# Weight loads in pieces of 4 KB per partition, in one pool of twelve buffers shared with the split's remainders

## The chip, the cores and the metric

The kernel runs on one core of a Trainium2 chip, in one launch. The metric is the device time of one execution in microseconds (us); the time of a kernel is the median of its runs. The engines are TensorE (PE in the profile; PEld is its weight load), VectorE (DVE), ScalarE (ACT), GpSimd (POOL) and SyncE (SP), which here does little but issue DMA transfers.

## The reference

Two layers act on 256 tokens of width 2048, with 256 tokens of context beside them in the first layer. Each layer first computes a modulation from the condition vector, the product of a silu vector with a 2048 by 6144 matrix, which yields a shift, a scale and a gate. Layer 0 projects to the parts of a gated linear attention and of a short convolution, mixes, and projects back; layer 1 projects to a pooled branch and a gate, mixes, and projects back. After each layer comes a normalised sum. Cut to that:

```
for i in range(2):
    sh, sc, gt = split(silu(c) @ w_ada[i] + b_ada[i], 3)        # (2048) @ (2048, 6144)
    u = x * (1 + sc) + sh                                       # (256, 2048)
    if i == 0:
        uc = ctx * (1 + sc_c) + sh_c                            # context, the same w_ada[0]
        s_f, s_b = context_states((uc @ w_in_e)[:, k, v, gates])
        y = even_mixer(u @ w_in_e, s_f, s_b, ...) @ w_out_e     # w_in_e (2048, 8224)
    else:
        xp, gate = split(u @ w_in_o, 2)                         # w_in_o (2048, 4096)
        z = einsum(window_mean(xp) - xp, w_pool) * pool_scale
        y = (z * silu(gate)) @ w_out_o
    x = layer_norm(sqrt(2) * x + gt * y)
```

All of it is fp32, with some 250 MB of weights that are each read once.

## The kernel before

**Products.** An fp32 product is made of three matmuls of rounded operands: `mm3` (lines 188 to 192) multiplies wh by uh (L190), the remainder wl by uh (L191) and wh by ul (L192). A weight therefore goes through three steps. `load_unit` (L135) loads a unit of four k-tiles of 128 rows by 512 columns, 1 MB, into one buffer `raw` of 8 KB per partition (L138, on the SP queue). `split_unit` (L143) cuts it in halves of two k-tiles: ScalarE casts a half to `wh` (L152), VectorE subtracts to get the remainder `wl` (L153). Then TensorE has 12 matmuls of 128x512 for each half and each block of tokens. For a few units marked wide the halves go to other buffers, `swh` and `swl`.

**Buffers.** `wraw` has 4 buffers of 8 KB per partition, one for each unit whatever its size, `whp` 4 of 4 KB and `wlp` 4 of 4 KB. A load into a buffer waits until the last reader of the unit four back is done.

**Order.** The list `specs` holds all units in the order of their use. `w_next` hands out the parts of the next one, and through `w_ahead` and `w_load` has the units behind it loaded (two ahead) and split (one ahead). Each engine's order is that of a list scheduler, which places instructions by priority and by its own idea of when each can start, the state of the pools included. The order below is therefore that of the built programs.

**Modulation.** The rows of layer 0 that are needed first are made on TensorE, straight from fp32 weights: `mod_rows` (L263) loads 1 MB units of `w_ada` and multiplies the silu vector with each k-tile (L274, tile `ada`). All other parts of the modulation are made on VectorE: `ada_unit` (L479) loads a 1 MB unit of `w_ada`, and `ada_accum` adds its four k-tiles, times a scalar, to `aacc` (L532 the first, L534 the others). These units use the same buffers `raw` and run through the whole kernel, a few at a time between blocks of the products (`pump_ada`).

**Stages.** Nine stages of one or two k-tiles each (`STAGES`) load modulation rows, make u, and multiply with the key columns (`stage_u`, `stage_k`, `v_fill`). Then come the rest of `w_in_e` (tile `xacc`, with the attention and the convolution in the background), `w_out_e` (`oacc`), layer 1 (`w_in_o`, `w_pool`), and `w_out_o`. Two places matter below. L966 on VectorE scales an attention output `y` that TensorE then transposes (L974, tile `yT`). L1333 multiplies a gate by a pooled branch, and TensorE transposes the result (L1286, tile `y1T`).

Of the kernel before, what the change touches and what calls it, by code (L numbers as in the profile page):

```python
# [9 lines left out]
F32 = mybir.dt.float32  # L10
F32R = mybir.dt.float32r
I32 = mybir.dt.int32
AF = mybir.ActivationFunctionType
ALU = mybir.AluOpType
# [3 lines left out]
P = 128  # L18
D = 2048
KT = D // P  # L20
SEQ = 256
NSLOT = 31
TAU = 16.0
EPS = 1e-5
ALPHA = math.sqrt(2.0)
# [5 lines left out]
KRAW = False  # L31
# [29 lines left out]
def kernel(  # L61
# [24 lines left out]
    nc = tc.nc  # L86
    names = {}

    def nm(s):
        names[s] = names.get(s, 0) + 1  # L90
        return f"{s}_{names[s]}"

    cpool = ctx.enter_context(tc.tile_pool(name="cpool", bufs=1))
    wraw = ctx.enter_context(tc.tile_pool(name="wraw", bufs=4))
    whp = ctx.enter_context(tc.tile_pool(name="whp", bufs=4))
    wlp = ctx.enter_context(tc.tile_pool(name="wlp", bufs=4))
    s4p = ctx.enter_context(tc.tile_pool(name="s4p", bufs=NSLOT))
    accp = ctx.enter_context(tc.tile_pool(name="accp", bufs=4, space=PSUM))
    mpp = ctx.enter_context(tc.tile_pool(name="mpp", bufs=4, space=PSUM))
# [9 lines left out]
    def const(shape, dt, name):  # L109
        return cpool.tile(shape, dt, tag=name, name=name)  # L110

    def slot(shape, dt=F32, name="s"):
        return s4p.tile(shape, dt, tag="s4", name=nm(name))

    def mp(shape, name="mp"):
        return mpp.tile(shape, F32, tag="mp", name=nm(name))
# [4 lines left out]
    def raw_tile(shape, name="raw"):  # L121
        return wraw.tile(shape, F32, tag="raw", name=nm(name))
# [10 lines left out]


    def load_unit(src, k0, nk, n0, nw=512):  # L135
        small_ = KRAW and nk * nw <= 1024
        r = slot([P, nk, nw], F32, "kraw") if small_ else raw_tile([P, nk, nw])
        nc.sync.dma_start(  # L138
            r, src[k0 * P : (k0 + nk) * P, n0 : n0 + nw].rearrange("(k p) n -> p k n", p=P)
        )  # L140
        return r

    def split_unit(r, nk, wide=False):  # L143
        parts = []
        for j in range(0, nk, 2):
            w = min(2, nk - j)
            if wide:
                h, l = slot([P, w, 512], F32R, "swh"), slot([P, w, 512], F32R, "swl")
            else:
                h = whp.tile([P, w, 512], F32R, tag="wh", name=nm("wh"))  # L150
                l = wlp.tile([P, w, 512], F32R, tag="wl", name=nm("wl"))
            nc.scalar.copy(h, r[:, j : j + w, :])  # L152
            nc.vector.tensor_tensor(out=l, in0=r[:, j : j + w, :], in1=h.bitcast(F32), op=ALU.subtract)  # L153
            for i in range(w):
                parts.append((h[:, i, :], l[:, i, :]))
        return parts
# [3 lines left out]
    wide = set()  # L160
# [70 lines left out]
    sil = const([P, KT, 34], F32, "sil")  # L231
# [31 lines left out]
    def mod_rows(k0, n):  # L263

        nw = n * P
        ps = mp([P, nw], "ada")
        nk = 2048 // nw
        for half, c0 in ((0, D + k0 * P), (1, k0 * P)):
            for kk in range(0, KT, nk):
                r = load_unit(w_ada[0], kk, nk, c0, nw)  # L270
                for j in range(nk):
                    kt = kk + j
                    g = kt % 4
                    nc.tensor.matmul(  # L274
                        out=ps[32 * g : 32 * g + 32, :], lhsT=sil[:, kt, 2 - 2 * half : 34 - 2 * half], rhs=r[:, j, :],
                        start=half == 0 and kt < 4, stop=half == 1 and kt >= KT - 4,
                    )
        return ps
# [37 lines left out]
    k0 = 0  # L316
# [35 lines left out]
    for s in ODD:  # L352
        g = int(s[1])
# [125 lines left out]
    def ada_unit(layer, k0, n0):  # L479

        if not ADA_SLOT:
            r = load_unit(w_ada[layer], k0, 4, n0)
            return [r[:, j, :] for j in range(4)]
        q = {"s": nc.sync, "g": nc.gpsimd}[ADA_SLOT]
        parts = []
        for k in (k0, k0 + 2):
            r = slot([P, 2, 512], F32, "araw")
            q.dma_start(r, w_ada[layer][k * P : (k + 2) * P, n0 : n0 + 512].rearrange("(k p) n -> p k n", p=P))
            parts += [r[:, 0, :], r[:, 1, :]]
        return parts  # L490
# [75 lines left out]
    prev, k0 = None, 0  # L566
# [135 lines left out]
    def gate_gen():  # L702
# [8 lines left out]
        for hp in range(2):  # L711
            res = {}
            for d in range(2):
# [22 lines left out]
                for half in range(2):  # L736
# [19 lines left out]
                    yield 1800  # L756
                nc.scalar.activation(e, e, AF.Exp, scale=-1.0 / TAU)
                nc.vector.tensor_tensor(out=e, in0=e, in1=kTc[hp], op=ALU.mult)
# [43 lines left out]
    def gla_gen(hp):  # L802
# [7 lines left out]
        def exps(t):  # L810
            nc.scalar.activation(t, t, AF.Exp, scale=-1.0 / TAU)

# [3 lines left out]
        def sub(o, a, b):  # L816
            nc.vector.tensor_tensor(out=o, in0=a, in1=b, op=ALU.subtract)
# [70 lines left out]
        sub(ch(kb), ch(gb)[:, :, 0:1].to_broadcast([P, 16, 64]), ch(gb))  # L888
        nc.scalar.activation(gl, gf[:, :, 63::64], AF.Exp, scale=-1.0 / TAU)
        nc.scalar.activation(bl, gb[:, :, ::64], AF.Exp, scale=-1.0 / TAU)  # L890
        for t, w in ((kf, kt_), (kb, kt_), (gf, qt), (gb, qt)):
# [169 lines left out]
    for i in range(2):  # L1061
        n0 = i * 512
        u = slot([P, 2, 512], F32, "ca")
        g = slot([P, 2, 512], F32, "cg")
# [237 lines left out]
    for s in ODD:  # L1302
        g = int(s[1])
# [84 lines left out]
```

## Time and profile before

| | |
|---|---|
| time, median of 3 runs | 1009.52 us (1008.19 to 1010.95) |
| profiled execution | 1010.29 us, of which the span from first to last instruction is 1008.5 us |
| mean granted clock of TensorE | 0.991 |
| busy in the span: PE, DVE, ACT | 960.9, 801.6, 469.3 us |
| moved by DMA | 255.44 MB, 253 GB/s in the mean |
| q1, the queue of SP | 72.4% of the time of 16 DMA engines |

Busy is the time in which an engine has an instruction running; what is left of the span is waiting. The chain that ended last is followed back from the last instruction, at each step to what released it. "[2.54 <-DMA raw<-in_w_ada_dram]" behind a row means that the engine stood idle for 2.54 us before it, until a transfer into `raw` had landed. The DMA share is the mean busy share of 16 DMA engines; transfers that overlap on an engine can take it above 1.

### The profile page before, as it was taken

The page shows a single profiled execution, that of the slowest core. Times are in us where ns is not written, and L with a number is a line of the kernel's source. Part 1 is how long each engine was busy: PE and PEld are TensorE (multiplying, and loading weights), DVE is VectorE, ACT ScalarE, POOL GpSimd, SP SyncE. Part 2 cuts the span into 40 slices and gives each one's busy share as a digit, 9 for nine tenths or more (in the row PEclk, how much of TensorE's full clock was granted, in tenths as well). Part 3 has the DMA queues.
Part 4 walks back from the last instruction along what each step waited for, and adds up shares of the span by engine and source line. Part 5 has one row for each costly group of instructions (what it writes and reads, how often), then busy time and mean ns, then how long its engine had stood idle before and what let it go on. Part 6 is the DMA issues. An engine that isn't in the chain of part 4 may idle for free.

```text
span 1008.5 us, 14323 instructions
## 1 busy us (share of the span) xinstructions
PE 960.9 (95%) x5654; PEld 759.2 (75%) x5654; DVE 801.6 (79%) x1142; ACT 469.3 (47%) x643; POOL 24.4 (2%) x56
## 2 busy tenths in 40 slices
PE   5899999999999999999999899999999999989995
PEld 4566656778878877887878778888778778778885
DVE  1555546979996999779999688897979997666676
ACT  2422214356675676236454344445745555435340
POOL 2000000000000000000000000000010001000000
PEclk9999999999999999999999999999999999999998
DMA  9977889566787586867767877985497999875532
GB/s 265 329 263 262 276 284 336 193 243 231 258 302 252 188 269 219 257 206 274 241 228 234 284 255 247 353 298 207 152 368 275 304 334 322 278 266 203 174 119 83
DMA packets 150371, 255.44 MB, mean 253 GB/s; under 512 B 5078, under 2 KB 46720, under 8 KB 150304
## 3 DMA queue, kind: packets, MB, share of 16 engines
q1 hardware_dynamic: 146592, 245.13, 72.4%
q0 software_dynamic: 2896, 8.72, 2.7%
q10 hardware_dynamic: 816, 0.68, 0.3%
q8 instruction: 44, 0.72, 0.3%
q14 instruction: 23, 0.19, 0.0%
HBM read 252.41 MB, written 2.10 MB: 252 GB/s over the span
## 4 chain that ended last, share of the span: by engine, by line
PE 41%; DVE 33%; DMA 18%; issue 5%; ACT 3%; SPq 0%; DVEq 0%; ACTq 0%
DMA raw<-in_w_ada_dram 15%; DVE wl L153 11%; DVE aacc L534 9%; PE oacc L191 5%; PE oacc L192 5%; PE oacc L190 5%; DMA raw<-in_w_in_o_dram 3%; PE xacc L192 3%; PE xacc L191 3%; PE xacc L190 3%; PE ada L274 2%; PE kacc L190 2%; PE kacc L192 2%; PE kacc L191 2%; PE pr L406 1%
## 5 line engine op out<-in xcount | busy, mean ns | idle before, releaser
L152 ACT CAST wh<-raw 128x1024 fp32r<-128x1024 f32 (+1 forms) x250 | 257.0, 1044 | 252.6 <-PE xacc L192 77.9
L153 DVE TENSOR_TENSOR wl<-raw,wh 128x1024 fp32r<-128x1024 f32 (+1 forms) x250 | 297.3, 1210 | 49.3 <-ACT wh L152 47.1
L534 DVE SCALAR_TENSOR_TENSOR aacc<-raw,sil,aacc 128x512 f32<-128x512 f32 x240 | 179.0, 747 | 34.2 <-DMA raw<-in_w_ada_dram 30.7
L190 PE MATMUL xacc<-wh,uxh 128*128 128x512 f32 x384 | 153.8, 400 | 0.0
L191 PE MATMUL xacc<-wl,uxh 128*128 128x512 f32 x384 | 150.9, 393 | 0.9 <-DVE wl L153 0.9
L192 PE MATMUL xacc<-wh,uxl 128*128 128x512 f32 x384 | 151.1, 394 | 0.0
L191 PEld LDWEIGHTS xacc<-wl,uxh 128*128 128x128 f32 x384 | 72.6, 189 | 17.3 <-DVE wl L153 1.7
L190 PEld LDWEIGHTS xacc<-wh,uxh 128*128 128x128 f32 x384 | 72.5, 189 | 15.6 <-issue 0.5
L192 PEld LDWEIGHTS xacc<-wh,uxl 128*128 128x128 f32 x384 | 72.4, 188 | 15.6 <-issue 0.2
L426 DVE TENSOR_TENSOR knat<-kacc,knat 128x512 f32<-128x512 f32 x64 | 42.8, 685 | 35.8 <-PE kacc L192 35.6
L285 ACT COPY arow<-ada 128x256 f32<-128x256 f32 (+1 forms) x9 | 3.1, 349 | 101.9 <-PE ada L274 101.9
L274 PE MATMUL ada<-raw,sil 128*32 128x256 f32 (+1 forms) x576 | 36.2, 380 | 12.0 <-DMA raw<-in_w_ada_dram 12.0
L190 PE MATMUL xacc<-wh,u1h 128*128 128x512 f32 x112 | 44.8, 400 | 0.8 <-ACT u1h L1167 0.8
L190 PE MATMUL oacc<-wh,y1h 128*128 128x512 f32 (+1 forms) x120 | 45.5, 379 | 0.0
L192 PE MATMUL oacc<-wh,y1l 128*128 128x512 f32 (+1 forms) x120 | 45.0, 375 | 0.0
L191 PE MATMUL oacc<-wl,y1h 128*128 128x512 f32 (+1 forms) x120 | 45.0, 375 | 0.0
L191 PE MATMUL xacc<-wl,u1h 128*128 128x512 f32 x112 | 44.1, 394 | 0.3 <-DVE wl L153 0.3
L192 PE MATMUL xacc<-wh,u1l 128*128 128x512 f32 x112 | 44.0, 393 | 0.0
L274 PEld LDWEIGHTS ada<-raw,sil 128*32 128x32 f32 x576 | 17.0, 118 | 28.6 <-issue 12.3
L190 PE MATMUL kacc<-wh,uxh 128*128 128x512 f32 x64 | 26.8, 418 | 1.5 <-ACT uxh L398 1.5
L1228 PE MATMUL xacc<-wh,dm 128*128 128x512 f32 x64 | 26.2, 409 | 1.6 <-ACT wh L152 1.6
L190 PE MATMUL kacc<-wh,uch 128*128 128x512 f32 x64 | 26.4, 412 | 0.5 <-DVE knat L426 0.5
(339 smaller groups left out, 1865.0 us busy)
## 6 DMA issues: line engine op xcount, KB each, us to landing
raw<-in_w_ada_dram SPq DMA_DIRECT2D x96, 1024.0 KB, 6.3
raw<-in_w_in_e_dram SPq DMA_DIRECT2D x54, 1024.0 KB, 6.0
raw<-in_w_in_o_dram SPq DMA_DIRECT2D x32, 1024.0 KB, 7.1
raw<-in_w_out_e_dram SPq DMA_DIRECT2D x16, 1024.0 KB, 6.7
raw<-in_w_out_o_dram SPq DMA_DIRECT2D x16, 1024.0 KB, 5.1
raw<-in_w_in_e_dram SPq DMA_DIRECT2D x18, 512.0 KB, 7.2
raw<-in_w_pool_dram SPq DMA_DIRECT2D x4, 1024.0 KB, 7.5
gt<-in_b_ada_dram POOLq DMA_DIRECT2D x8, 256.0 KB, 3.8
```

The source lines that it names most:

```text
L152: nc.scalar.copy(h, r[:, j : j + w, :])
L153: nc.vector.tensor_tensor(out=l, in0=r[:, j : j + w, :], in1=h.bitcast(F32), op=ALU.subtract)
L190: nc.tensor.matmul(out=acc, lhsT=uh, rhs=wh, start=start, stop=False)
L191: nc.tensor.matmul(out=acc, lhsT=uh, rhs=wl, start=False, stop=False)
L192: nc.tensor.matmul(out=acc, lhsT=ul, rhs=wh, start=False, stop=stop)
L274: nc.tensor.matmul(out=ps[32 * g : 32 * g + 32, :], lhsT=sil[:, kt, 2 - 2 * half : 34 - 2 * half], rhs=r[:, j, :], start=half == 0 and kt ...
L285: arow_ins.append(nc.scalar.copy(a[:, :nw], ps))
L406: nc.tensor.matmul(out=pr[32 * g : 32 * g + 32, :], lhsT=wr[:, kk, :], rhs=quad_u[kk // 2][:, kk % 2, :], start=True, stop=True,)
L426: nc.vector.tensor_tensor(out=dst, in0=acc, in1=dst, op=ALU.add)
L534: e.scalar_tensor_tensor(out=a, in0=r[j], scalar=sc, in1=a, op0=ALU.mult, op1=ALU.add)
L1228: nc.tensor.matmul(out=accs[0], lhsT=dh, rhs=wh, start=f, stop=False)
```

## The change

A load unit is cut into pieces of 1024 elements (4 KB) per partition, 512 KB each; each piece has a buffer of its own and a DMA of its own. `wraw` holds 12 such buffers instead of 4 of 8 KB. The pool `wlp` is gone: remainders `wl` take buffers of `wraw`, under the same tag, so that pieces and remainders follow one another through the same twelve. The memory is the same, 48 KB per partition. `split_unit` casts and subtracts a piece as it did a half, in instructions of the same shapes and number; `mod_rows` and `ada_unit` find their k-tiles in the pieces. A unit of one or two k-tiles of 512 columns (256 or 512 KB, in the stages) stays one piece. SP issues 482 DMAs instead of 265. Line numbers of the changed kernel are 2 or 3 higher.

```
-    wraw = ctx.enter_context(tc.tile_pool(name="wraw", bufs=4))
+    wraw = ctx.enter_context(tc.tile_pool(name="wraw", bufs=NRAW))      # NRAW = 12
     whp = ctx.enter_context(tc.tile_pool(name="whp", bufs=4))
-    wlp = ctx.enter_context(tc.tile_pool(name="wlp", bufs=4))
...
     def load_unit(src, k0, nk, n0, nw=512):
-        small_ = KRAW and nk * nw <= 1024
-        r = slot([P, nk, nw], F32, "kraw") if small_ else raw_tile([P, nk, nw])
-        nc.sync.dma_start(
-            r, src[k0 * P : (k0 + nk) * P, n0 : n0 + nw].rearrange("(k p) n -> p k n", p=P)
-        )
-        return r
+        w = 1024 // nw
+        pieces = []
+        for k in range(k0, k0 + nk, w):
+            n = min(w, k0 + nk - k)
+            r = raw_tile([P, n, nw])
+            nc.sync.dma_start(r, src[k * P : (k + n) * P, n0 : n0 + nw].rearrange("(k p) n -> p k n", p=P))
+            pieces.append((r, n))
+        return pieces
...
-    def split_unit(r, nk, wide=False):
+    def split_unit(pieces, nk, wide=False):
         parts = []
-        for j in range(0, nk, 2):
-            w = min(2, nk - j)
+        for r, w in pieces:
...
-                l = wlp.tile([P, w, 512], F32R, tag="wl", name=nm("wl"))
-            nc.scalar.copy(h, r[:, j : j + w, :])
-            nc.vector.tensor_tensor(out=l, in0=r[:, j : j + w, :], in1=h.bitcast(F32), op=ALU.subtract)
+                l = wraw.tile([P, w, 512], F32R, tag="raw", name=nm("wl"))
+            nc.scalar.copy(h, r)
+            nc.vector.tensor_tensor(out=l, in0=r, in1=h.bitcast(F32), op=ALU.subtract)
...
 # mod_rows
-                r = load_unit(w_ada[0], kk, nk, c0, nw)
+                r = [p[:, i, :] for p, w in load_unit(w_ada[0], kk, nk, c0, nw) for i in range(w)]
...
-                        ... rhs=r[:, j, :],
+                        ... rhs=r[j],
...
 # ada_unit
-            r = load_unit(w_ada[layer], k0, 4, n0)
-            return [r[:, j, :] for j in range(4)]
+            return [p[:, i, :] for p, w in load_unit(w_ada[layer], k0, 4, n0) for i in range(w)]
```

With other loads and other buffers the scheduler also orders the engines anew. Three places show it; the order on TensorE, VectorE and ScalarE differs in many more.

TensorE in the early stages, where `mod_rows` takes its units; `ada` is the modulation of one stage, `kacc` the key columns. Before, in the fourth of the two-k-tile stages:

```order
L274 MATMUL ada_883<-raw_884,sil 32x256 x8
L274 MATMUL ada_883<-raw_894,sil 32x256 x8
L190 MATMUL kacc_954<-wh_870,uxh_120 128x512
L191 MATMUL kacc_954<-wl_871,uxh_120 128x512
L192 MATMUL kacc_954<-wh_870,uxl_121 128x512
```

and now, at the end of the same stage's modulation:

```order
L277 MATMUL ada_912<-raw_939,sil 32x256 x4
L194 MATMUL kacc_1047<-wl_906,uch_119 128x512
L195 MATMUL kacc_1047<-wh_905,ucl_120 128x512
L277 MATMUL ada_912<-raw_949,sil 32x256 x4
L277 MATMUL ada_912<-raw_951,sil 32x256 x4
L291 MATMUL adaT_963<-sel_101,arow_961 128x4 x2
```

A row "x8" was one unit, two of them stood together at the head of a stage. Now a piece is "x4", and the first five or six pieces of a stage stand apart, with three to five matmuls of 128x512 between them; the uninterrupted runs of such rows are 40 instead of 26.

VectorE in the last part of the attention, where the norm's root (`rst`, `rsy`) is followed by `y` (before):

```order
L1015 TENSOR_TENSOR rsy_2_4885<-rsy_2_4885,rst_2_4884 128x4
L534 SCALAR_TENSOR_TENSOR aacc_10_4985<-raw_5082,sil,aacc_10_4985 128x512
L966 SCALAR_TENSOR_TENSOR y_4859<-po_4861,rsy_2_4885,gs_2936 128x256 x2
L966 SCALAR_TENSOR_TENSOR y_4859<-po_4872,rsy_2_4885,gs_2936 128x256
L153 TENSOR_TENSOR wl_5040<-raw_5000,wh_5039 128x1024
L153 TENSOR_TENSOR wl_5044<-raw_5000,wh_5043 128x1024
L966 SCALAR_TENSOR_TENSOR y_4859<-po_4872,rsy_2_4885,gs_2936 128x256
```

and now:

```order
L1016 TENSOR_SCALAR rst_2_5113<-rst_2_5113 128x4
L1017 TENSOR_TENSOR rsy_2_5114<-rsy_2_5114,rst_2_5113 128x4
L968 SCALAR_TENSOR_TENSOR y_5088<-po_5090,rsy_2_5114,gs_3073 128x256 x2
L968 SCALAR_TENSOR_TENSOR y_5088<-po_5101,rsy_2_5114,gs_3073 128x256 x2
L980 SCALAR_TENSOR_TENSOR ybl_5087<-yT_5265,colT,ybh_5086 128x2x128
L156 TENSOR_TENSOR wl_5332<-raw_5286,wh_5331 128x1024
L980 SCALAR_TENSOR_TENSOR ybl_5087<-yT_5265,colT,ybh_5086 128x2x128
L536 SCALAR_TENSOR_TENSOR aacc_10_5220<-raw_5323,sil,aacc_10_5220 128x512 x2
```

The first k-tile of a `w_ada` unit stood ahead of `y`; now two remainders stand within the root's steps, and the k-tiles of `w_ada` behind `y`.

VectorE in layer 1, at the second of three gates multiplied by a pooled branch (before):

```order
L153 TENSOR_TENSOR wl_7382<-raw_7345,wh_7381 128x1024
L153 TENSOR_TENSOR wl_7418<-raw_7385,wh_7417 128x1024
L534 SCALAR_TENSOR_TENSOR aacc_16_7330<-raw_7471,sil,aacc_16_7330 128x512
L153 TENSOR_TENSOR wl_7422<-raw_7385,wh_7421 128x1024
L1333 TENSOR_TENSOR gate_7258<-gate_7258,pooled_7039 128x1024
L534 SCALAR_TENSOR_TENSOR aacc_16_7330<-raw_7471,sil,aacc_16_7330 128x512 x2
```

and now:

```order
L536 SCALAR_TENSOR_TENSOR aacc_16_7715<-raw_7716,sil,aacc_16_7715 128x512
L536 SCALAR_TENSOR_TENSOR aacc_16_7715<-raw_7718,sil,aacc_16_7715 128x512 x2
L156 TENSOR_TENSOR wl_7769<-raw_7732,wh_7768 128x1024
L1335 TENSOR_TENSOR gate_7639<-gate_7639,pooled_7406 128x1024
L156 TENSOR_TENSOR wl_7773<-raw_7734,wh_7772 128x1024
L536 SCALAR_TENSOR_TENSOR aacc_16_7715<-raw_7760,sil,aacc_16_7715 128x512 x2
```

The k-tile of a new unit (`raw_7471`) stood ahead of the gate; now the gate stands ahead of the new unit's first piece (`raw_7760`), behind one remainder.

## Rows read from the trace of the kernel before

**Rows 1.** The page: busy time of each engine, and the chain that ended last by line.

```profile
PE 960.9 (95%) x5654; PEld 759.2 (75%) x5654; DVE 801.6 (79%) x1142; ACT 469.3 (47%) x643; POOL 24.4 (2%) x56
...
DMA raw<-in_w_ada_dram 15%; DVE wl L153 11%; DVE aacc L534 9%; PE oacc L191 5%; PE oacc L192 5%; PE oacc L190 5%; DMA raw<-in_w_in_o_dram 3%; PE xacc L192 3%; PE xacc L191 3%; PE xacc L190 3%; PE ada L274 2%; PE kacc L190 2%; PE kacc L192 2%; PE kacc L191 2%; PE pr L406 1%
```

**Rows 2.** Busy time by stretch: PE, PEld, DVE, ACT, POOL; clock, DMA share, GB/s.

```profile
25.00:50.00 25.00, 22.22 (x158) 13.40 (x147) 14.63 (x27) 10.44 (x21) 0.00 (x0) 1.00 1.02 329
50.00:75.00 25.00, 24.91 (x164) 17.14 (x164) 13.51 (x24) 6.63 (x12) 0.00 (x0) 1.00 0.79 263
582.00:584.00 2.00, 2.00 (x7) 1.61 (x6) 2.00 (x2) 1.67 (x2) 0.00 (x0) 0.50 0.01 2
800.00:850.00 50.00, 49.69 (x225) 40.36 (x223) 43.42 (x58) 26.73 (x33) 3.20 (x6) 1.00 0.97 345
```

**Rows 3.** What TensorE waited for: us in total, times, longest us.

```profile
PE ada L274 <- DMA raw<-in_w_ada_dram: 12.0, 6, 4.9
```

**Rows 4.** TensorE, early stages: start us, us, instruction, xcount [idle before, releaser].

```profile
12.14 1.28 PE L274 MATMUL ada<-raw,sil 128*32 128x128 f32 x17 [2.54 <-DMA raw<-in_w_ada_dram]
...
39.30 1.07 PE L274 MATMUL ada<-raw,sil 128*32 128x256 f32 x16 [1.84 <-DMA raw<-in_w_ada_dram]
...
105.11 1.07 PE L274 MATMUL ada<-raw,sil 128*32 128x256 f32 x16 [0.82 <-DMA raw<-in_w_ada_dram]
106.11 0.50 PE L191 MATMUL kacc<-wl,uxh 128*128 128x512 f32 x1
106.45 0.39 PE L192 MATMUL kacc<-wh,uxl 128*128 128x512 f32 x1
106.68 0.40 PE L190 MATMUL kacc<-wh,uxh 128*128 128x512 f32 x1
...
124.27 1.93 PE L274 MATMUL ada<-raw,sil 128*32 128x256 f32 x32
```

**Rows 5.** TensorE in order of time, around its three longest later waits.

```profile
581.29 0.99 PE L974 MATMUL yT<-ident,y 128*128 128x128 f32 x4 [5.14 <-DVE y L966]
581.93 0.78 PE L190 MATMUL xacc<-wh,uxh 128*128 128x512 f32 x1
...
585.00 0.40 PE L191 MATMUL xacc<-wl,uxh 128*128 128x512 f32 x1
...
747.04 0.50 PE L1228 MATMUL xacc<-wh,dm 128*128 128x512 f32 x1 [1.55 <-ACT wh L152]
...
748.63 0.52 PE L1232 MATMUL xacc<-wl,dm 128*128 128x512 f32 x1
...
752.28 0.40 PE L1231 MATMUL xacc<-wl,dm 128*128 128x512 f32 x1
...
888.80 1.97 PE L1286 MATMUL y1T<-ident,gate 128*128 128x128 f32 x8 [3.59 <-DVE gate L1333]
```

**Rows 6.** VectorE in order of time, at the first and the last of them.

```profile
580.00 0.75 DVE L534 SCALAR_TENSOR_TENSOR aacc<-raw,sil,aacc 128x512 f32<-128x512 f32 x1 [5.58 <-DMA raw<-in_w_ada_dram]
580.66 1.26 DVE L966 SCALAR_TENSOR_TENSOR y<-po,rsy,gs 128x256 f32<-128x256 f32 x3
...
885.73 0.75 DVE L534 SCALAR_TENSOR_TENSOR aacc<-raw,sil,aacc 128x512 f32<-128x512 f32 x1 [4.74 <-DMA raw<-in_w_ada_dram]
...
887.53 1.22 DVE L1333 TENSOR_TENSOR gate<-gate,pooled 128x1024 f32<-128x1024 f32 x1
```

**Rows 7.** Chain of waits in order of time: start us, us, what.

```profile
735.75 10.09 DMA raw<-in_w_in_o_dram
```

**Rows 8.** What the SP queue waited for, same columns as rows 3.

```profile
SPq L138 <- DVE wl L153: 452.5, 111, 16.7
```

**Rows 9.** SP in order of time: one DMA issue.

```profile
572.98 0.37 SPq L138 DMA_DIRECT2D raw<-in_w_in_e_dram  x1
```

**Rows 10.** DMA issues: count, KB each, median us from issue to landing.

```profile
raw<-in_w_out_o_dram SPq DMA_DIRECT2D x16, 1024.0 KB, 5.1
```

**Rows 11.** VectorE semaphore instructions of line 153: ns min/median/max.

```profile
L153 DVEq EVENT_SEMAPHORE  x161: 21/21/1483, 15.1 to 973.5; - x161
```

More of the change, by code (lines that the diff above doesn't have):

```diff
@@ L22 @@
 NSLOT = 31
+NRAW = 12
 TAU = 16.0
@@ L274, in mod_rows @@
                     nc.tensor.matmul(
-                        out=ps[32 * g : 32 * g + 32, :], lhsT=sil[:, kt, 2 - 2 * half : 34 - 2 * half], rhs=r[:, j, :],
+                        out=ps[32 * g : 32 * g + 32, :], lhsT=sil[:, kt, 2 - 2 * half : 34 - 2 * half], rhs=r[j],
                         start=half == 0 and kt < 4, stop=half == 1 and kt >= KT - 4,
```

## The prediction

> **What bounds the kernel now.** The page comes first. TensorE is busy for 960.9 us of a span of 1008.5, VectorE for 801.6 [rows 1], so at most 47.6 us can be had by waiting less. The chain by line names what the waiting is for: transfers of `w_ada` hold 15% of it, the subtraction for `wl` 11%, the accumulation `aacc` 9% [rows 1]. The windows then show where. Up to about 45 us the transfers are the limit: from 25 to 50 us the DMA share is 1.02 and TensorE is busy for 22.22 of 25 us; from 50 us on it is full, 24.91 of 25, at a share of 0.79 [rows 2]. Later the transfers fill up again in places, as from 800 to 850 us with 0.97 and 345 GB/s [rows 2].
>
> The waits of TensorE and the timeline give the rest. `mod_rows` waited 12.0 us, six times, for a unit of `w_ada` [rows 3]; the longest, 4.9, is the first load of all, 2.54 came at 12.14 us and 1.84 at 39.30 [rows 4]. That leaves 2.7 us for three later ones, of which 0.82 stands at 105.11 [rows 4]. Three waits are longer: 5.14 us at 581.29, 1.55 at 747.04, 3.59 at 888.80 [rows 5]. The first and the last have one cause, which VectorE's rows show: an `aacc` whose unit had not landed stands ahead of what TensorE needs. The root was done by 574.4, then VectorE waits 5.58 us, and only then comes `y` L966; before 885.73 it waits 4.74 us, and the gate L1333 stands behind [rows 6]. The one at 747 hangs on a unit of `w_in_o` that took 10.09 us to come [rows 7].
>
> Each of the three costs more than its idle time, for afterwards the granted clock is 0.50, 1.2 GHz instead of 2.4, as from 582 to 584 us [rows 2]. After the first the seven matmuls from 581.93 to 585.00 take 3.07 us, 0.44 each [rows 5], where 0.23 (106.45 to 106.68) is the pace at full clock [rows 4]: 7 x 0.21 = 1.5 us lost. After the second the nine from 748.63 to 752.28 take 3.65 instead of 2.07: 1.6 us. After the third the transposes go as slowly as after the first, 1.97 us for eight and 0.99 for four [rows 5]; I take 1.6 us as after the others. So the three together hold 5.14 + 1.55 + 3.59 = 10.3 us of idle time and 4.7 us of slow clock.
>
> **The change part by part.** *No work is added on the busy engines:* casts, subtractions and matmuls are the same in number and shape.
>
> *SP's issues.* 217 more, at 0.37 us each [rows 9], 80 us of SP's time. SP waits 452.5 us for `wl` alone [rows 8], so this is hidden, except where several pieces come free at once; at the start four pieces instead of two units cost two issues, under 0.8 us, while earlier transfers keep the engines of DMA full. I take 0.
>
> *The early stages.* A piece of 512 KB lets TensorE start when half a unit has landed. The total landed by 45 us does not change, so of the waits at the start I count 1 us (nothing to the 2.54 of [rows 4]). The three later ones, from 105 us on, hold the 2.7 us. There the stream is not full (the share is 0.79 from 50 us on), the order gives the pieces room (three to five matmuls of 0.23 us between two of them), and more of them fit in the pool: -2.4 us (0 to -2.7).
>
> *Switching between the two kinds of matmul.* A run of one unit (16 rows in the trace) takes 1.00 us from its start to the next matmul (105.11 to 106.11), a run of two is listed with 1.93 against 1.07 [rows 4], so the second unit adds 0.86: each run has 1.00 - 0.86 = 0.14 us of its own. The first matmul of the other kind takes 0.34 (106.11 to 106.45) instead of 0.23, another 0.11 [rows 4]. There are 40 runs instead of 26: 14 x 0.25 = +3.5 us, nothing if all of it falls into waiting, which it does not, as most stages lie behind 50 us.
>
> *581 us.* In the new order the `aacc` stands behind `y`; in its place two remainders (1.2 us each, as in [rows 6] the other operations of 128x1024) stand within the root's steps, and two blocks of `xacc` move ahead on TensorE. Both loss and slow clock, 6.6 us, would go; but the subtractions hang on loads of a stretch where transfers are late, and one earlier `aacc` still stands ahead of the root. I take -5 (0 to -6.6).
>
> *888 us.* The gate now stands ahead of the unit that it waited behind, with one subtraction before it: 3.59 + 1.6, I take -5 (0 to -5.2).
>
> *747 us.* The load of `w_in_o` is released by pieces and comes free earlier, as its buffer was last held by a whole unit of `w_ada` that VectorE read in four steps. But the stream is nearly full there, so half: -1.5 of 3.2 (0 to -3.2).
>
> *The shared pool.* In rotation a piece now often takes the buffer that a `wl` had, and waits until TensorE has read it, later than VectorE's last read. From the order, up to about 190 us the piece last in the same buffer is 9 or 10 pieces back, later 6 to 8, where four whole units were 8. So what can be under way in advance is more at first and up to a quarter less later. A transfer of 1 MB lands 5.1 us after issue where it is alone [rows 10], half of it in under that, and by the order TensorE has at least some thirty matmuls of 0.23 us, 7 us of work, between the release of a buffer and the use of what is loaded into it, in all cases but one after the start. I take +2 us for pieces that come late where the stream is full (0 to +8: 345 GB/s over 50 us [rows 2] are sixteen units of 1 MB, at half a us each).
>
> *Waits and semaphores.* The order shows 791 matmuls with a wait instead of 686. A wait that is over already costs nothing, one that holds a matmul up as in [rows 4] 0.11 us: 0 to 105 x 0.11 = 11.6; I take +2. VectorE gets about 160 semaphore instructions more, of 21 ns [rows 11]: 3.4 us, of which a third lies where VectorE sets the pace: +1.
>
> *New waits of the same kind.* The order has been made anew from end to end, and three bad places in about 800 us is what this scheduler left before. That the new one has none is not likely: +2 (0 to +8).
>
> The sum: -1 - 2.4 + 3.5 - 5 - 5 - 1.5 + 2 + 2 + 1 + 2 = -4.4 us. It stands against the profiled execution of 1010.29, which is 0.8 us above the median of 1009.52: 1009.5 - 4.4 = 1005.1, I say 1005.
>
> **What speaks against it.** In this trace 1 MB landed in 5.1 us at best [rows 10], and 345 GB/s were held over 50 us [rows 2] with 1 MB units for the most part; how 512 KB pieces do no row here shows in a stretch of their own. The Trainium skill, in "DMA: Bandwidth & Descriptors", section "Rules for kernel authors", asks for at least 1 MiB per DMA, and its section "Measured" has 32% of the peak for 64 KB against 78% for 1 MB. By that rule the change would lower the rate.
>
> **The rivals.** *(a) No change.* The stalls go, but what TensorE gains it loses again where VectorE or the stream sets the pace: the same bytes have to land by the same place. Up to there only one half of the 15 us goes, against 3.5 + 2 + 1 + 2 + 2 of costs. The time would be 1007 to 1012.5. For it speaks that transfers fill 0.97 of a stretch [rows 2], against it that TensorE is busy for 49.69 of 50 us there all the same [rows 2].
>
> *(b) Slower: the shared pool.* A buffer that a `wl` held is released by TensorE, so each TensorE delay passes to the load behind it, then to the cast, then to TensorE again. It decides once a piece lands over 1 us after its cast could start in the full stretches, about 700 to 900 us. Sixteen units in 50 us [rows 2] make some sixty in 200; 0.25 us lost on each is +15, less the 11 of the stalls, and +3.5 of switches: about 1017. For it: six pieces are less than eight. Against it: 7 us of work between release and use, and at most the 5.1 us of a whole unit for half of one [rows 10].
>
> *(c) Slower: smaller transfers move fewer bytes.* If the rate fell by a tenth where the stream is full, the first 45 us would take 4.5 us more and 700 to 900 us up to 10 more, with what the order gains lost in it: about 1016. It decides from a twentieth on. Against it: a piece has the same rows of 2 KB or 1 KB as its unit had, so only their count per DMA is halved.
>
> *(d) More.* All waits named go, nothing new comes: -2.5 - 2.7 - 6.6 - 5.2 - 3.2 + 3.5 = -16.7, about 993 to 999.
>
> **How the numbers follow.** 0.3% is 3 us, about what a measurement of this kernel can tell from no change: faster is below 1006.5, slower above 1012.5. My forecast (1000 to 1010 on its own) has 0.48, of which 0.36 lies below 1006.5 and 0.12 above; (d) and what lies between has 0.18; (a) 0.14; (b) 0.13; (c) 0.07. Faster is 0.36 + 0.18 = 0.54, the same 0.12 + 0.14 = 0.26, slower 0.20. The range leaves out a tenth on either side: the far half of (d) below 996, and the far half of (b) and (c) above 1016.
>
> **What would show it.** In the changed profile: no wait above 2 us of TensorE for `y` L968 at about 580 us, none for the gate L1335 at about 885, and the granted clock at 1.00 there; waits of `ada` L277 from 100 us on below 0.5 us in all; runs of four pieces' rows apart, 0.25 us each. If (b) holds, ScalarE's casts wait for transfers much longer than before in the second half, and SP waits for TensorE's L194 where it waited for `wl`. If (c) holds, the GB/s from 25 to 50 us fall below 329 at a share above 1. The prediction is wrong if a new wait on TensorE of over 5 us stands anywhere, or if the stretch from 800 to 900 us grows longer.

## The result, and the profile after

The changed kernel takes 1054.05 us (median of 4 runs, 1052.74 to 1055.84) against 1008.86 (4 runs): 1.0449 times the time before, 95% interval 1.042 to 1.0477. Its profiled execution takes 1053.12 us, with a span of 1051.3 and a mean granted clock of 0.981. The span has grown by 42.8 us.

The page of the changed kernel, its busy times and its chain by line:

```profile
PE 982.8 (93%) x5654; PEld 758.3 (72%) x5654; DVE 801.8 (76%) x1142; ACT 467.0 (44%) x643; POOL 24.5 (2%) x56
...
DVE wl L156 8%; DVE aacc L536 6%; PE xacc L194 6%; PE xacc L195 6%; PE xacc L193 6%; PE oacc L194 4%; PE oacc L195 4%; PE oacc L193 4%; PE kacc L193 3%; PE kacc L194 3%; PE kacc L195 3%; PE ada L277 3%; DMA raw<-in_w_ada_dram 2%; PE pcx L944 1%; PE po L962 1%
```

Against [rows 1], VectorE and ScalarE have the same work. TensorE, with the same matmuls, is busy for 21.9 us longer, and its idle time has grown from 47.6 to 68.5 us. The chain hardly runs through loads of `w_ada` any more.

TensorE's waits in the changed kernel (us in total, times, longest us):

```profile
PE ada L277 <- DMA raw<-in_w_ada_dram: 7.2, 6, 2.6
PE oacc L194 <- DVE wl L156: 6.4, 9, 1.3
PE xacc L194 <- DVE wl L156: 6.1, 10, 1.1
PE vfill L193 <- ACT swh L155: 5.7, 2, 2.8
PE xacc L1230 <- ACT dm L1186: 5.6, 1, 5.6
PE xT L1161 <- issue: 4.2, 1, 4.2
PE adaT L291 <- ACT arow L288: 3.8, 8, 0.5
...
PE y1T L1288 <- DVE gate L1326: 0.3, 2, 0.2
```

These rows answer to [rows 3] and [rows 5]. What was forecast to go has gone: `ada` waits 7.2 us, all of it before 40 us; `y1T` waits 0.3 for its gates; there is no row for `yT`. In their place stand rows that were not there, or hardly: `vfill` (the value columns made in the stages) for a cast, `adaT` (the transpose of the finished modulation) for ScalarE's copy of it, eight times instead of once, `xT` (the transposes of the normalised sum between the layers), `dm` (an operand of layer 1 that VectorE makes and ScalarE casts), and nineteen short waits of `oacc` and `xacc` for `wl`. The 5.64 us at `dm` is a new wait of over 5 us, which the prediction had named as a sign that it is wrong.

The same waits in order of time on TensorE (start us, us, instruction [idle before, releaser]):

```profile
129.13 1.22 PE L193 MATMUL vfill<-swh,uxh 128*128 128x512 f32 x2 [2.83 <-ACT swh L155]
...
153.85 0.64 PE L277 MATMUL ada<-raw,sil 128*32 128x256 f32 x8
154.98 0.39 PE L291 MATMUL adaT<-sel,arow 128*128 128x4 f32 x2 [0.49 <-ACT arow L288]
...
604.90 0.30 PE L976 MATMUL yT<-ident,y 128*128 128x128 f32 x1
...
725.75 2.79 PE L1161 MATMUL xT<-ident,xr 128*128 128x128 f32 x12 [4.21 <-issue]
...
748.41 0.79 PE L1230 MATMUL xacc<-wh,dm 128*128 128x512 f32 x1 [5.64 <-ACT dm L1186]
```

`yT` at 604.90 follows without a wait ([rows 5] had 5.14 us there). The second row is the last piece of a stage's modulation and the third the transpose that needs its result: with nothing put between them, TensorE waits for ScalarE's copy. The wait of 2.83 us at 129.13 begins in the same way. Two rows of ScalarE and, for `dm`, one of VectorE show what the longer waits stand behind:

```profile
124.33 0.37 ACT L288 COPY arow<-ada 128x256 f32<-128x256 f32 x1 [20.55 <-PE ada L277]
...
128.02 1.05 ACT L155 CAST swh<-raw 128x1024 fp32r<-128x1024 f32 x1
```

```profile
742.09 0.49 DVE L534 TENSOR_SCALAR aacc<-raw,sil 128x512 f32<-128x512 f32 x1 [2.80 <-DMA raw<-in_w_ada_dram]
```

ScalarE stood idle for 20.55 us until the last piece of the stage's modulation was multiplied; the cast `swh`, which `vfill` needs, stands behind the copy `arow` and the stage's `u` in its order. TensorE has only `adaT` and the transposes `px` left by then, and runs out of work. At 742.09 an `aacc` whose piece had not landed stands ahead of the operation that `dm` needs: the kind of wait of [rows 6], at a new place.

By stretch (columns as in [rows 2]; 45 to 214.4 us are the stages up to the rest of the value columns, tile `vacc`):

```profile
25.00:50.00 25.00, 21.86 (x198) 13.97 (x189) 13.22 (x26) 9.18 (x19) 0.00 (x0) 1.00 1.08 355
45.00:214.40 169.40, 159.21 (x928) 100.74 (x928) 92.21 (x155) 40.63 (x71) 0.41 (x2) 0.96 0.73 232
129.00:134.00 5.00, 4.87 (x12) 3.81 (x13) 2.99 (x3) 1.97 (x3) 0.00 (x0) 0.50 0.83 244
725.00:750.00 25.00, 17.77 (x82) 14.06 (x83) 18.67 (x35) 18.20 (x40) 0.00 (x0) 0.85 0.27 88
800.00:850.00 50.00, 46.47 (x203) 35.03 (x202) 44.41 (x61) 25.34 (x34) 1.06 (x2) 1.00 0.81 265
```

and the stages of the kernel before, which end at 198.9 us:

```profile
45.00:198.90 153.90, 150.46 (x946) 101.40 (x945) 97.39 (x173) 42.85 (x77) 0.41 (x2) 1.00 0.83 267
```

From 25 to 50 us the pieces move 355 GB/s, more than the 329 of [rows 2]: the transfers are not slower. The stages take 169.4 us instead of 153.9, 15.5 more. TensorE is idle in them for 169.4 - 159.2 = 10.2 us instead of 3.4, and busy for 8.8 us longer at a mean granted clock of 0.96: with the wait that ended at 129.13 us it went to 1.2 GHz (0.50 in the row). An estimate from the 0.96, with the two levels 1.00 and 0.50: 13.6 of the 169.4 us at half clock, of which half, 6.8 us, are lost. From 725 to 750 us, at the boundary of the layers, TensorE is busy for 17.77 of 25 us. From 800 to 850 us it is busy for 46.47 us instead of 49.69, while the transfers move 265 GB/s instead of 345 [rows 2].

The SP queue's waits, with the columns of [rows 8]:

```profile
SPq L142 <- DVE wl L156: 234.3, 120, 11.9
SPq L142 <- PE xacc L195: 131.1, 59, 16.3
SPq L142 <- DVE aacc L536: 97.4, 59, 5.4
SPq L142 <- PE xacc L194: 61.0, 28, 5.5
...
SPq L142 <- PE oacc L195: 30.6, 16, 6.8
```

Before, SP waited 452.5 us for `wl`; now it waits for `wl` half as long, and much longer for TensorE. L194 reads a remainder. L195 reads no buffer of this pool, and stands behind L194 in TensorE's order; that its rows mean the same wait is inferred.

Where the 42.8 us lie, by the first matmul of each part on TensorE: 15.5 in the stages; 3.1 from there to the first `oacc` (409.9 instead of 406.8 us); 24.2 from the first `oacc` to the end (427.0 instead of 402.8).

### The profile page after: what moved, and what is told of

The parts are those of the page before. It is cut to its first block, busy times and chain, and to the rows that moved or that the text cites. A ratio compares the mean times of both kernels' runs of the same rounds, so it can differ in the third digit from the quotient of the medians.

```text
span 1051.3 us, 14862 instructions
## 1 busy us (share of the span) xinstructions
PE 982.8 (93%) x5654; PEld 758.3 (72%) x5654; DVE 801.8 (76%) x1142; ACT 467.0 (44%) x643; POOL 24.5 (2%) x56
## 4 chain that ended last, share of the span: by engine, by line
PE 60%; DVE 25%; issue 7%; ACT 4%; DMA 2%; SPq 0%; DVEq 0%; ACTq 0%
DVE wl L156 8%; DVE aacc L536 6%; PE xacc L194 6%; PE xacc L195 6%; PE xacc L193 6%; PE oacc L194 4%; PE oacc L195 4%; PE oacc L193 4%; PE kacc L193 3%; PE kacc L194 3%; PE kacc L195 3%; PE ada L277 3%; DMA raw<-in_w_ada_dram 2%; PE pcx L944 1%; PE po L962 1%
## 5 line engine op out<-in xcount | busy, mean ns | idle before, releaser
L194 PE MATMUL xacc<-wl,uxh 128*128 128x512 f32 x384 | 152.9, 398 | 5.4 <-DVE wl L156 5.0
L195 PE MATMUL xacc<-wh,uxl 128*128 128x512 f32 x384 | 150.3, 392 | 0.0
L193 PE MATMUL xacc<-wh,uxh 128*128 128x512 f32 x384 | 149.7, 398 | 0.3 <-ACT wh L155 0.3
L194 PEld LDWEIGHTS xacc<-wl,uxh 128*128 128x128 f32 x384 | 72.1, 188 | 25.7 <-DVE wl L156 10.7
L195 PEld LDWEIGHTS xacc<-wh,uxl 128*128 128x128 f32 x384 | 72.1, 188 | 14.9 <-issue 0.5
L194 PE MATMUL oacc<-wl,y1h 128*128 128x512 f32 (+1 forms) x120 | 45.1, 379 | 3.0 <-DVE wl L156 3.0
L277 PE MATMUL ada<-raw,sil 128*32 128x256 f32 (+1 forms) x576 | 38.8, 379 | 7.2 <-DMA raw<-in_w_ada_dram 7.2
L194 PE MATMUL xacc<-wl,u1h 128*128 128x512 f32 x112 | 44.2, 396 | 1.2 <-DVE wl L156 1.1
L195 PE MATMUL oacc<-wh,y1l 128*128 128x512 f32 (+1 forms) x120 | 44.7, 376 | 0.0
L195 PE MATMUL xacc<-wh,u1l 128*128 128x512 f32 x112 | 43.5, 390 | 0.0
L193 PE MATMUL xacc<-wh,u1h 128*128 128x512 f32 x112 | 42.8, 400 | 0.6 <-DVE xr L1158 0.5
L193 PE MATMUL oacc<-wh,y1h 128*128 128x512 f32 (+1 forms) x120 | 42.8, 376 | 0.0
L1088 DVE TENSOR_TENSOR arow<-oacc,gt 128x512 f32<-128x512 f32 (+1 forms) x17 | 11.1, 655 | 37.6 <-PE oacc L195 37.6
L277 PEld LDWEIGHTS ada<-raw,sil 128*32 128x32 f32 x576 | 14.6, 114 | 26.4 <-issue 10.1
```

The costliest lines, as they stand in the source:

```text
L193: nc.tensor.matmul(out=acc, lhsT=uh, rhs=wh, start=start, stop=False)
L194: nc.tensor.matmul(out=acc, lhsT=uh, rhs=wl, start=False, stop=False)
L195: nc.tensor.matmul(out=acc, lhsT=ul, rhs=wh, start=False, stop=stop)
L277: nc.tensor.matmul(out=ps[32 * g : 32 * g + 32, :], lhsT=sil[:, kt, 2 - 2 * half : 34 - 2 * half], rhs=r[j], start=half == 0 and kt < 4, s ...
L1088: nc.vector.tensor_tensor(out=t, in0=accs[nb][m + (cs.start > 0)][:, cs], in1=gt[nb // 2][:, nb % 2, cs], op=ALU.mult)
```

## The experiments

The theory after the first look was that the shared pool makes the scheduler write a worse order, and that this order loses the time. The rivals: the buffers themselves do it, as loads wait for TensorE through the shared rotation; or the smaller transfers do.

**Taking the change apart.** First, pieces with remainders of their own:

```
-NRAW = 12
+NRAW = 8
...
+    wlp = ctx.enter_context(tc.tile_pool(name="wlp", bufs=4))
...
-                l = wraw.tile([P, w, 512], F32R, tag="raw", name=nm("wl"))
+                l = wlp.tile([P, w, 512], F32R, tag="wl", name=nm("wl"))
```

> Pieces as in the changed kernel (512 KB, 4 KB buffers, 482 DMAs), but the remainders have their own pool again: 8 buffers for pieces, 4 for wl, the same 48 KB. Its order has 27 runs of ada on TensorE (26 before, 40 changed), the root's and layer boundary's order of before (23 oacc matmuls between the first and the last xT; 0 in the changed kernel). If the shared pool is to blame, by the order that it causes or by its waits: 1003 to 1013 us, most of the 45 us gone. If the smaller transfers or their number are: over 1035.

Measured: 1020.22 us, 1.0116 times before (1.0083 to 1.0149). Three quarters of the loss are gone with the sharing, a quarter is not: the time lies in neither of the two ranges. SP's waits, and the two longest waits of TensorE from 600 us to the end:

```profile
SPq L143 <- DVE wl L157: 388.8, 207, 17.3
SPq L143 <- DVE aacc L537: 145.4, 114, 4.5
```

```profile
PE y1T L1289 <- DVE gate L1327: 5.7, 1, 5.7
PE adaS L558 <- DVE cv L1058: 4.9, 1, 4.9
```

SP waits for VectorE again. The two waits are for operations of VectorE, as two of those of [rows 5] were, at other places.

Second, the kernel before with two DMAs for each unit, into one buffer:

```
-        nc.sync.dma_start(
-            r, src[k0 * P : (k0 + nk) * P, n0 : n0 + nw].rearrange("(k p) n -> p k n", p=P)
-        )
+        w = 1024 // nw
+        for j in range(0, nk, w):
+            n = min(w, nk - j)
+            nc.sync.dma_start(
+                r[:, j : j + n, :], src[(k0 + j) * P : (k0 + j + n) * P, n0 : n0 + nw].rearrange("(k p) n -> p k n", p=P)
+            )
```

> The kernel before, its pools untouched, but each load of 1 MB as two DMAs of 512 KB into the two halves of the same buffer. If smaller transfers are to blame: over 1035 us. If the shared pool is: 1003 to 1013, with the DMA rate from 25 to 50 us at 320 GB/s or more.

Measured: 1003.9 us, 0.9942 (0.9925 to 0.9959): 0.6% less, in an interval that leaves out 1. Two stretches of it:

```profile
25.00:50.00 25.00, 24.00 (x162) 13.81 (x161) 14.82 (x27) 11.65 (x23) 0.00 (x0) 1.00 1.01 323
800.00:850.00 50.00, 50.00 (x228) 41.02 (x227) 44.05 (x57) 28.44 (x34) 3.20 (x6) 1.00 0.99 346
```

323 and 346 GB/s at about the shares of [rows 2]: at this size the smaller transfers cost nothing. That the early landing of half a unit gains the 6 us is likely, but not separated from the order, which is new here too (34 runs of `ada` instead of 26). The Trainium skill, "DMA: Bandwidth & Descriptors", section "Rules for kernel authors", asks for at least 1 MiB per DMA for the most bandwidth; these rows do not bear that out for 512 KB against 1 MB.

Third and fourth, the changed kernel with one buffer more or less (`NRAW = 13`, `NRAW = 11`):

> The changed kernel with 13 buffers in the shared pool instead of 12. Its order on TensorE has the same marks as with 12 (40 ada runs, adaT right behind the last ada piece in 8 stages, 0 oacc between the xT). If the order is what costs: 1045 to 1058 us. If buffers are too few, so that loads wait: one more is a sixth of what the pieces have beyond the wl, 1030 to 1044.

> The changed kernel with 11 buffers. If the order is what costs: 1045 to 1060 us, as its marks are the same. If buffers are too few: 1065 to 1090.

Measured: 1054.83 us with 13 (1.0449, 1.0421 to 1.0477) and 1063.48 with 11 (1.0538, 1.0514 to 1.0562). In the traces TensorE's order with 13 differs from that with 12 at 52 of 5654 matmuls, and the time does not differ. One more buffer does not help as long as the order stays. With 11 the order differs at 293, and the time lies between the two ranges, so its 9 us say nothing on their own.

**Order against buffers.** The order of one engine can be fixed without touching anything else, by edges that only order the issue. `_want` holds TensorE's instructions in the order of the other kernel's program; the other engines are scheduled around it. "Own order" is below the order of the run with own remainders, "changed order" that of the changed kernel:

```
for _a, _b in zip(_want, _want[1:]):
    tc.add_manual_dep(_b, _a.name, mybir.DependencyInfo(mybir.DependencyClass.NoSync, mybir.DependencyReason.DATA), reason="issue order")
```

All of TensorE, both ways:

> The buffers of the run with own remainders (8 for pieces, 4 for wl; 1020 us), but TensorE's instructions in the order of the changed kernel, instruction for instruction; the other engines are scheduled around it. If TensorE's order carries the loss: 1045 to 1060 us, with waits behind the last oacc (xT) and at the first dm as in the changed kernel. If the shared buffers carry it by their waits: 1015 to 1028.

> The changed kernel, twelve shared buffers, but TensorE's instructions in the order of the run with own remainders. If TensorE's order carries the loss: 1015 to 1030 us. If the shared buffers carry it by their waits: 1045 to 1065, with waits of TensorE for casts and remainders in place of those behind the stages.

Measured: 1069.11 us (1.0575, 1.0529 to 1.062) and 1063.4 us (1.0526, 1.0495 to 1.0558). Each theory was right where it forecast a loss (the first loses 9 us more than its range) and wrong where it forecast none: the order loses by itself, and the buffers lose with the other order. In the second run the part between `vacc` and the first `oacc` alone takes 428.4 us, where the changed kernel needs 409.9. The whole kernel is too large a unit for the question, so the next runs fix a part only. TensorE's first 900 instructions, up to `vacc`:

> The changed kernel, shared buffers, with only TensorE's first 900 instructions (up to the rest of the value columns, which start at 214.4 us there) in the order of the run with own remainders. If that order costs the 15.5 us which the stages lost: vacc starts at 199 to 204 us and the time is 1037 to 1045. If the buffers' waits do: vacc at 210 or later and 1049 to 1058. If what is gained there is given back behind: vacc early, and still over 1049.

Measured: 1040.27 us (1.0309, 1.0278 to 1.0339), 14 us less than the changed kernel. And the mirror image, the own buffers with the changed kernel's order in that part:

> The run with own remainders (1020 us), with only TensorE's first 884 instructions in the order of the changed kernel. If that order costs the stages' loss by itself: 1034 to 1045 us, vacc at 212 to 222 instead of 198.5. If it costs only together with shared buffers: 1017 to 1027.

Measured: 1040.53 us (1.0312, 1.0273 to 1.035), 20 us more than with the own order. The stretch from 45 us to `vacc` in the run with own remainders, in the shared buffers with its order, and in the own buffers with the changed order:

```profile
45.00:198.50 153.50, 150.50 (x946) 101.75 (x944) 97.45 (x173) 42.95 (x77) 0.41 (x2) 1.00 0.86 276
```

```profile
45.00:198.80 153.80, 151.73 (x949) 102.43 (x948) 95.72 (x170) 43.92 (x78) 0.41 (x2) 1.00 0.84 269
```

```profile
45.00:223.90 178.90, 164.16 (x946) 104.09 (x945) 99.85 (x173) 44.72 (x77) 0.41 (x2) 0.94 0.77 240
```

Four cells: own order 153.5 us with own and 153.8 with shared buffers; changed order 178.9 with own and 169.4 with shared buffers. The clock is 1.00 in the first two and 0.94 in the third. What was gained there also came out at the end (14 us of 15.6).

The second cell scatters. Three other runs have the same buffers and the same order of TensorE in this part, and their stretch takes 154.7 us (the stages and the boundary of the layers fixed), 157.2 (all of TensorE, above) and 161.6 (the stages and all from the first `oacc` on). In the last of them all engines have, up to `vacc`, the same instructions in the same order as in the run with 153.8:

```profile
45.00:206.60 161.60, 158.10 (x949) 104.41 (x949) 96.22 (x170) 44.36 (x79) 0.41 (x2) 0.96 0.80 255
```

```profile
165.72 1.03 PE L277 MATMUL ada<-raw,sil 128*32 128x256 f32 x8 [1.82 <-DMA raw<-in_w_ada_dram]
```

A wait of 1.82 us and three of some 0.4 behind it stand where the other execution waited twice, 0.85 us at most, and here the clock fell. So one execution can differ from another by 8 us in this stretch. The order's 15.6 and 25.4 us stand clear of that: in the stages TensorE's order is the cause, with either buffers. A cost of the buffers with the own order does not show beyond the scatter.

The boundary of the layers, TensorE's 466 instructions from the first `oacc` to the last `xT`, and then both parts:

> The changed kernel with only TensorE's 466 instructions from the first oacc to the last xT (the boundary of the layers) in the order of the run with own remainders. If the order there costs what that stretch lost: the waits of 4.2 and 5.6 us at xT and dm go, and 1041 to 1048 us. If remainders come late there because of the buffers, whatever the order: 1050 to 1058.

> Both stretches at once. If the two losses are separate and of the order: 1026 to 1037 us, the sum of the two gains. If the shared buffers set the time in the end: 1045 or more.

Measured: 1055.43 us (1.0451, 1.0414 to 1.0489) and 1038.31 us (1.0291, 1.0261 to 1.0321). The second lies in neither range; it is 2 us below the run with the stages alone, in intervals that overlap, so that order is worth nothing that can be told. TensorE's waits in the boundary's order, from 624 to 790 us:

```profile
PE oacc L194 <- DVE wl L156: 4.0, 5, 1.5
PE oacc L193 <- ACT wh L155: 2.2, 1, 2.2
PE xacc L1233 <- DVE wl L156: 2.0, 1, 2.0
PE xT L1161 <- issue: 1.6, 1, 1.6
```

The 5.6 us at `dm` are gone and the 4.2 at `xT` are 1.6, but remainders and casts are waited for, and from the first `oacc` to the first `zT` (a transpose in layer 1) it takes 161 us as against 160 in the changed kernel. In the shared buffers the own order gains nothing here, whatever the reason.

Everything from the first `oacc` to the end, both ways:

> The run with own remainders, with TensorE's order from the first oacc to the end as in the changed kernel. If the late loss is of TensorE's order: 1032 to 1045 us. If it is of the shared buffers: 1017 to 1027.

> The changed kernel with TensorE's early stages and all from the first oacc to the end in the order of the run with own remainders (early alone gave 1040). If the late loss is of TensorE's order: 1020 to 1030 us. If the shared buffers make loads late there: 1036 to 1050, with casts and remainders waited for.

Measured: 1039.45 us (1.0312, 1.0261 to 1.0364) and 1042.18 us (1.0316, 1.0273 to 1.0359; it has the early order too, so its measure is 1040.27). From the first `oacc` to the end of the span: 415.2 us with own buffers and own order, 431.1 with own buffers and the changed order, 429.7 with shared buffers and own order, 427.0 in the changed kernel. Other runs with the same order on TensorE in this part repeat the first three: 412.4 us (the run with the changed order in the stages only), 425.9 and 429.9 (the two with all of TensorE fixed). Late, then, the own order gains nothing in the shared buffers. SP's waits from 605 us on, with shared buffers and own order, and four of TensorE's:

```profile
SPq L142 <- PE oacc L195: 91.0, 32, 8.1
SPq L142 <- DVE wl L156: 57.4, 36, 5.7
SPq L142 <- PE xacc L195: 54.7, 18, 16.1
SPq L142 <- PE xacc L1234: 41.0, 22, 4.1
```

```profile
PE oacc L194 <- DVE wl L156: 5.8, 7, 1.5
PE gtb L523 <- DVE aacc L536: 5.4, 1, 5.4
PE xacc L1233 <- DVE wl L156: 4.8, 4, 2.0
PE pacc L194 <- DVE wl L156: 3.2, 2, 2.4
```

SP waits 91.0 us for `oacc` and 54.7 for `xacc` on TensorE, where in the run with own remainders VectorE's `wl` was the first row, and TensorE waits for remainders. That would fit loads that come late for the casts, but ScalarE's waits in the same stretch do not show it. The first two rows are of this run, the third is the longest wait of a cast for a transfer in the run with own remainders:

```profile
ACT wh L155 <- PE oacc L195: 75.7, 38, 8.6
ACT wh L155 <- DMA raw<-in_w_out_e_dram: 14.0, 6, 4.5
```

```profile
ACT wh L156 <- DMA raw<-in_w_in_o_dram: 21.5, 11, 5.3
```

From the first `oacc` to the end all casts wait for transfers for 26.9 us in this run and 20.2 in the changed kernel, but 35.5 before and 34.8 with own remainders; VectorE's `aacc` waits 1.2 and 2.8 us for them, against 18.2 and 27.8. So SP's waits for TensorE are there, but pieces that come late for their readers are not. The casts wait above all for TensorE to free a buffer of `wh`. By which wait the shared buffers make this part longer is not shown.

**Size of transfers and of the pool.**

> The kernel before, with each load of 1 MB as four DMAs of 256 KB into the quarters of its buffer (two DMAs gave 1003.9 us). If smaller transfers cost rate anywhere, this shows it: over 1010 us and fewer GB/s from 25 to 50 us. If early landing is what counts: 998 to 1005, 47 runs of ada instead of 34 costing up to 3 us of it.

Measured: 1024.84 us (1.0161, 1.0118 to 1.0204); the edit is `w = 512 // nw` in the code of the two DMAs. Its start and its stages:

```profile
25.00:50.00 25.00, 23.76 (x147) 11.90 (x146) 11.90 (x23) 9.31 (x19) 0.00 (x0) 1.00 0.88 281
45.00:214.20 169.20, 166.15 (x964) 105.32 (x963) 100.61 (x179) 46.01 (x82) 0.41 (x2) 1.00 0.80 256
```

281 GB/s at a share of 0.88 from 25 to 50 us, and 169.2 us for the stages; the page has TensorE busy for 53.2 us in `ada` instead of 36.2, its rows stretched as quarter after quarter comes in. As forecast for smaller transfers that cost, the time is over 1010 us and the rate lower; but whether the rate fell because of the size, or because the order asked for less, was not separated.

> Own remainders, with 9 buffers for pieces instead of 8. If the 16 us between this layout and two DMAs into whole units come from too few buffers: 1008 to 1015 us. If they come from an order with a few bad places: anything within 1012 to 1026, with its own longest waits.

Measured: 1031.82 us (1.022, 1.0176 to 1.0264), with `NRAW = 9` and own remainders. That is above both ranges: a ninth buffer for pieces makes the kernel 12 us slower than eight. The loss lies between `vacc` and the first `oacc`, 416.6 us instead of 401.6. Too few buffers are thus not what separates 1020 from 1004 us. That the order which the scheduler finds does it is likely and was not tested.

> The kernel before, with two DMAs per unit for w_ada alone; the units of the other weights as before. If the early landing of w_ada halves is the gain of 6 us: 1002 to 1007 us. If the weights' halves are: 1008 to 1012.

Measured: 1005.6 us (0.9966, 0.994 to 0.9992); only units of `w_ada` are loaded by two DMAs (`w = nk` for the others). The gain is smaller than with all units halved, and the two intervals overlap, so how it divides stays open. The lowest median of all versions is that with two DMAs for every unit, 1003.9 us.

## Why the prediction was wrong

Forecast was 1005 us, in a range of 996 to 1016, with 0.20 for slower; measured 1054.05.

- **SP's issues, nothing.** Right: with as many DMAs into the buffers of before, the kernel takes 1003.9 us.
- **The early stages, -1 and -2.4.** The three waits from 105 us on are gone and `ada` waits 7.2 us instead of 12.0. The row was right, its neighbourhood was not looked at.
- **The switches, +3.5, and the waits and semaphores, +2 and +1.** None was measured alone. In the stages TensorE is busy for 8.8 us longer, of which the estimate above gives 6.8 to the half clock; some 2 us are left for switches.
- **581, 888 and 747 us.** `yT` and the gates wait no more, as forecast, and no `wh` is waited for at the place of 747; but there `dm` waits 5.64 us, behind an `aacc` on VectorE that waited for its piece.
- **The shared pool, +2 us (0 to +8).** Mis-sized. In the stages no cost of it shows beyond the scatter. Late, with the same order on TensorE, the part takes 429.7 against 415.2 us, 14.5 more. The price was put on pieces that come late; SP waits for TensorE as in the 91.0 us above, but late pieces are not what the casts and `aacc` show (26.9 and 1.2 us of waiting for transfers, against 34.8 and 27.8). What the 14.5 us consist of stays open. The 5.1 us of [rows 10], which the prediction calls the best, are a median.
- **New waits of the same kind, +2 (0 to +8).** This is the step that failed first. The reasoning was "three bad places in about 800 us is what this scheduler left before", a mean for places not read. The new order was read only where the old one had waits, so each of them could only improve. The stages alone lost 15.5 us by their order, and the rows stood in the part on the change: two pieces of `ada` with `adaT` right behind them. In the trace before, two or three matmuls of `kacc` stood between at seven of nine stages; in the changed one they stand there at none. Those rows were priced for the switch (0.25 us a run), not for the waits of what now follows (`adaT`, and `vfill` for a cast behind the copy), nor for the half clock behind them.
- **Rival (b)**, with 1017 us, named two signs. SP does wait for TensorE where it waited for `wl`; the casts do not wait longer for transfers in the second half, but less. So its chain from load to cast to TensorE is not borne out, and it had nothing for the stages' order. **Rival (c)** falls: two DMAs per unit are faster, and the pieces moved 355 GB/s.

The account of the 42.8 us of span: 15.5 by TensorE's order in the stages, shown from both sides. Of the 24.2 from the first `oacc` on, 12.4 remain with own remainders: TensorE is idle for 29.2 us in that part instead of 20.5 before, and busy for 3.8 us longer. The two rows shown hold 10.6 us of that idle time. The other 11.8 go with the shared buffers, whichever of the two orders TensorE has; that the order is adapted to them is a guess. The 3.1 between were not pursued. That fixing TensorE alone leaves the other engines to be scheduled around it blurs the late part: orders of all engines together could not be exchanged, and whether some order would be fast in the shared buffers was not tried.

## What to carry to other kernels

When buffers change under a scheduler, compare the new order along its whole length and price what now stands directly behind its producer, not only the places where the old trace had waits. To tell an order from the buffers that caused it, fix the order of one engine in one stretch with the other layout's buffers, both ways; one more buffer (1054.8) or a layout in between (1020.2, 1031.8) does not tell them apart. A pool that a late reader shares with a load makes the load wait for that reader (131.1 and 61.0 us of SP's time); what this costs has to be read from those who wait for the load, here the casts, and not from SP. Loading half a unit at a time into the same buffer did without the sharing (1003.9 us).

## What was not expected of the hardware

That a wait is followed by half the clock was in the prediction; its share was not expected. A wait of 2.83 us that ended at 129.13 us went with a granted clock of 0.50 from 129 to 134 us, and over half of the stages' growth is TensorE being busy more slowly (8.8 of 15.5 us, the switches between matmuls among them), not waiting. Nor was the scatter expected: the same instructions in the same order reached `vacc` at 198.8 us in one execution and at 206.6 in another, in which the clock of the stages was 0.96 instead of 1.00 behind waits of 1.82 us and less. And 256 KB transfers moved 281 GB/s from 25 to 50 us, where 512 KB ones moved 323 to 355; size and order are not separated there.
